# Copies of weight sums on the other DMA queue, an earlier biased input and a tile of its own for the centred block

## The chip, the cores and the metric

The kernel runs on one core of a Trainium2 chip. The metric is the device time of one execution in microseconds (us). Before the change three runs gave 747.36, 748.40 and 749.13 us; the median is 748.4. TensorE (PE) multiplies matrices, VectorE (DVE) and ScalarE (ACT) do the elementwise work, GpSimd (POOL) does little arithmetic here and issues DMAs, and SyncE (SP) only issues DMAs. SP's DMAs go through the queue that the profile calls q1 (hardware_dynamic), POOL's through q0 (software_dynamic).

## The reference

One layer on an input x of 1024 steps by 1024 channels, all in float32:

```python
h = x @ w_in + b_in                        # split: xa, za, xb, zb, ga, gb
xa = causal_depthwise_conv4(xa)
ya = rg_lru(xa) * silu(za)                 # two block-diagonal gates, a scan over time
yb = multi_scale_pool(xb) * silu(zb)       # running means, a projection per group
merged = sigmoid(ga) * (ya @ w_proj_a) + sigmoid(gb) * (yb @ w_proj_b)
y = merged @ w_out + b_out
out = layer_norm(alpha * x + y) * ln_gain + ln_bias     # alpha = 2 ** 0.25
```

## The kernel before

**The products.** The input projection, the two merge projections and the output projection are each done as a two by two block scheme with seven block products instead of eight (Strassen's, in Winograd's form). Such a scheme needs sums of weight blocks and of input blocks. Each operand is split into a high and a low part by a cast on ACT (names ending in h) and a difference on DVE (names ending in l), and each block product is three matmul passes: high by high, low by high, high by low.

**The stages.** The first stage goes over 24 groups of the input projection, the list `order` of L601 to L604: G0, A0, G1 to A5, G6, A6, A7, G7 (the branch A is the recurrence, G are the merge gates), then B0 to B7 (the pooling). A group loads its weights (tiles ra and rb), casts them (wah, wal and so on), multiplies (PSUM tiles a, c, e) and hands its results on. A further small weight, gr, 64 KB, holds the gates' blocks of an A group: it is loaded by SP (`load_g`) and cast to gh on ACT and gl on DVE. The branches' outputs ya and yb are stored to DRAM. Next come the merge products (PSUM tiles pa, pc and pe; `load` at L1231 fetches weights such as wa1r and inputs such as xa1r, `cast` at L1241 splits them into oh and ol), and last the output products (oa, oc, oe) with the norm. In the output phase eight blocks of 128 rows, zt[s] (z in the profile), are loaded from DRAM tiles xb, which hold x + b_out / alpha; `o_add` (L1419) adds each product to them and `o_norm` (L1433) normalises each block.

**Sums in DRAM.** Sums that only feed later loads are made in DRAM by DMA, without an engine: `summed` (L673) makes a tile by a copy of the first term and one accumulating DMA for each further term (`add_to`, L670; accumulation always goes through POOL). It serves `weight_sums` (p1a to p4a and p1b to p4b), `output_sums` (L690; p1o to p4o, four tiles of 1 MB with one copy and one addition each), and `input_sums1` and `input_sums2` (t1 to t4 of each branch). `biased_input` (L702) does the same for xb: two halves of the bias row go to SBUF, are multiplied by 1 / alpha on ACT and stored to a DRAM row; then four tiles xb of 1 MB get a copy of x and the addition of the broadcast row. All copies and additions are issued by POOL.

**When they are issued.** Each copy and each addition is a job in the list `jobs`. After each group from the third on, `run_jobs` (L663) pops two jobs (three in B groups). It first lets ACT copy one column of that group's last result (pace) and POOL copy that (paced), so that POOL goes on only when the group is there. A DMA that needs another's result waits for it at its issue, and holds what POOL issues behind it. `output_sums` and the first input sums are appended when ya's first half is complete, `input_sums2("a")` and `biased_input` after the last A group.

**The order.** The engines' programs are not written in the order of the code: `Plan` (L162 to L392) collects all operations, gives each a due time worked back from PE's order, and lays out the engines' programs from estimated durations. PE and POOL keep the written order. SP, ACT and DVE are sorted by due time; SP issues a load at most 25 us (LEAD) ahead of its due time. What runs is fixed by these orders and by semaphores. All operations are emitted at L394, so the profile tells them apart by tiles alone.

Of the kernel before, what the change touches and what calls it, by code (L numbers as in the profile page):

```python
# [11 lines left out]
F32 = mybir.dt.float32  # L12
F32R = mybir.dt.float32r
AF = mybir.ActivationFunctionType
ALU = mybir.AluOpType
# [391 lines left out]
def layer_kernel(ctx: ExitStack, tc: tile.TileContext, xq, x, w_in, par, wg, w_pool, wpa, wpb, w_out, rows, out):  # L407
# [235 lines left out]
    def both(t, m1):  # L643
        for sl in HALF:
            V.tensor_tensor(t[:, sl], t[:, sl], m1, ALU.add)
# [17 lines left out]
    def run_jobs(n, i=None, t=None):  # L663
        if jobs and i is not None:
            A.copy(pace[:, i:i + 1], t[:, 0:1])
            nc.gpsimd.tensor_copy(paced[:, i:i + 1], pace[:, i:i + 1])
        for _ in range(min(n, len(jobs))):
            jobs.pop(0)()

    def add_to(t, u):  # L670
        nc.gpsimd.dma_start(t, u, accum_op=ALU.add, max_dma_last_dim=2048)

    def summed(name, *terms):  # L673
        t = dram.tile([KQ, P, H], F32, tag=name, name=name)
        jobs.append(lambda: nc.gpsimd.dma_start(t, terms[0]))
        for u in terms[1:]:
            jobs.append(lambda: add_to(t, u))
        return t

    def weight_sums(n, w):  # L680
        a11, a12, a21, a22 = (w[KQ * i:KQ * i + KQ, :, KQ * k:KQ * k + KQ, :].rearrange("n p k m -> n p (k m)")
                              for i in range(2) for k in range(2))
        p1 = summed(f"p1{n}", a21, a22)
        p3 = summed(f"p3{n}", a11, a21)
        p2 = summed(f"p2{n}", a11, p1)
        src["w", n] = {1: a11, 2: a12, 4: a22, 5: p1, 6: p2, 7: p3, 3: summed(f"p4{n}", a12, p2)}
# [3 lines left out]
    def output_sums():  # L690
        a11, a12, a21, a22 = (w_out[H * k:H * (k + 1), H * i:H * (i + 1)].rearrange("(q p) n -> q p n", p=P)
                              for i in range(2) for k in (1, 0))
        p1 = summed("p1o", a21, a22)
        p3 = summed("p3o", a11, a21)
        p2 = summed("p2o", a11, p1)
        src["w", "o"] = {1: a11, 2: a12, 4: a22, 5: p1, 6: p2, 7: p3, 3: summed("p4o", a12, p2)}


    xb_d = [dram.tile([2 * P, D], F32, tag=f"xb{i}", name=f"xb{i}") for i in range(4)]
    bias_d = dram.tile([1, D], F32, tag="bias", name="bias")  # L700

    def biased_input():  # L702
        for sl in HALF:
            t = epool.tile([1, H], F32, tag="e", name=f"bias_{sl.start}")
            nc.sync.dma_start(t, rows[0:1, sl])
            A.mul(t, t, 1.0 / ALPHA)
            nc.sync.dma_start(bias_d[:, sl], t)
        for i in (2, 3, 0, 1):
            jobs.append(lambda i=i: nc.gpsimd.dma_start(xb_d[i], x[2 * P * i:2 * P * (i + 1), :]))
            jobs.append(lambda i=i: add_to(xb_d[i], bias_d.to_broadcast((2 * P, D))))  # L710


    def input_sums1(n):
# [46 lines left out]
    def a_gates(c, xc, xh, xl, sz):  # L760
        gh, gl = gw[c]
        if c + 1 < NK:
            load_g(c + 1)

        r, i = kt(f"r{c}"), kt(f"i{c}")
        for h in range(2):
            pg = [bank(f"ps_g{c}_{h}_{n}") for n in range(2)]
            for k, (w, m) in enumerate(((gh, xh), (gh, xl), (gl, xh))):
                for n in range(2):
                    nc.tensor.matmul(pg[n], w[HEAD[n], :], m[HEAD[n], HALF[h]], start=k == 0, stop=k == 2)  # L770
            for t, half, ps, s, cb in ((r, LO, pg[0], LO, C_BR), (r, HI, pg[1], HI, C_BR),
                                       (i, LO, pg[0], HI, C_BI), (i, HI, pg[1], LO, C_BI)):
                A.activation(t[half, HALF[h]], ps[s], AF.Sigmoid, bias=par_sb[s, cb + c:cb + c + 1])

        a = kt(f"a{c}")
        A.activation(a, r, AF.Exp, scale=sc_a[:, c:c + 1])
        t = r
        A.activation(t, r, AF.Tanh, scale=sc_t[:, c:c + 1])
        V.tensor_tensor(i, i, xc, ALU.mult)
        V.scalar_tensor_tensor(i, a, 1.0, i, ALU.add, ALU.mult)  # L780
        V.scalar_tensor_tensor(a, a, 1.0, t, ALU.add, ALU.mult)
        V.tensor_scalar(a, a, -1.0, 1.0, ALU.mult, ALU.add)
        A.activation(t, t, AF.Sqrt)
        V.tensor_tensor(i, i, t, ALU.mult)
        hs = t
        V.tensor_tensor_scan(hs, a, i, 0.0, ALU.mult, ALU.add)
        V.tensor_tensor(hs, hs, sz, ALU.mult)
        A.mul(hs[:, negative(c)], hs[:, negative(c)], -1.0)
        store_y("a", c, hs)
        if c == KQ - 1:  # L790
            input_sums1("a")
            output_sums()
        elif c == NK - 1:
            input_sums2("a")
            biased_input()


    sg_d = {sec: dram.tile([NK, P, S], F32, tag=f"sg{sec}", name=f"sg{sec}") for sec in (GA, GB)}
# [349 lines left out]
    due, pools, last, ends, W = {}, {}, [], [], {}  # L1148
    weight_sums("a", wpa)
    weight_sums("b", wpb)  # L1150
    for i in range(1, len(order)):
        kind, c = order[i]
        if i == 1:
            W[2] = load_group(2, w_next, ("4", "75", "63"))
        elif i + 1 < len(order):
            W[i + 1] = load_group(i + 1)
        if kind == "B" and c % 2 == 1:
            load_wp(c // 2)
        if i == 1:
            tiles = tiles0  # L1160
        elif kind == "A":
            tiles, takes = a_outputs(c)
        elif kind == "B":
            tiles, takes = b_outputs(c)
        else:
            finish, takes = g_outputs(GA if c < 4 else GB, c % 4)
        if i > 1:
            g = Group(f"{kind}{c}", W.pop(i), X, *takes)

        def heads(at=pools):  # L1170
            for f in at.pop(i, []):
                f()

        def between():
            heads(due)
            if prev_m3:
                prev_m3()
            if prev_end and i > 2:
                prev_end()

        if i == 1:
            prev_m3 = None
        elif i >= len(order) - 2:
            g.sums(between, heads)
            prev_m3 = None
            last.append(g)
        else:
            g.m1()
            g.m2()
            if i == 2:  # L1190
                rest = first_rest()
                next(rest)
            g.m7()
            between()
            g.m6()
            if i == 2:
                next(rest)
                prev_end()
            g.m4()
            heads()  # L1200
            g.m5()
            prev_m3 = g.m3
        if i >= 2:
            run_jobs(3 if kind == "B" else 2, i, g.t7)
        if kind == "A":
            def prev_end(c=c, tiles=tiles, i=i):
                front = a_front(c, *tiles)
                due.setdefault(i + 2, []).append(lambda: a_gates(c, *front, tiles[1]))
        elif kind == "B":
            def prev_end(c=c, tiles=tiles, i=i):  # L1210
                for _ in b_front(c, *tiles):
                    pass
                if c % 2 == 1:
                    pools.setdefault(i + 2, []).append(lambda: b_pool(c // 2))
        else:
            prev_end = finish
        if i >= len(order) - 2:
            ends.append((c, *tiles))
            prev_end = None
# [213 lines left out]
    def o_norm(s):  # L1433
        sd = const.tile([P, 1], F32, name=f"sd{s}")
        sls = [slice(e * H, (e + 1) * H) for e in range(2)]
        if s == last:
            mv = const.tile([P, 2], F32, name=f"mv{s}")
            V.bn_aggr(mv, stats)
            A.activation(sd, mv[:, 1:2], AF.Sqrt, bias=eps)
            mean, op = mv[:, 0:1], ALU.subtract  # L1440
        else:
            nm, var = (const.tile([P, 1], F32, name=f"{n}{s}") for n in ("nm", "var"))
            V.tensor_scalar(nm, acc[:, 2 * s:2 * s + 1], acc[:, 2 * s + 1:2 * s + 2], -1.0 / D, ALU.add, ALU.mult)
            sq = kt(f"sq{s}")
            A.activation(sq, zt[s], AF.Square, bias=nm, accum_out=var)
            A.activation(sd, var, AF.Sqrt, bias=eps, scale=1.0 / D)
            mean, op = nm, ALU.add
        for sl in sls:
            V.scalar_tensor_tensor(zt[s][:, sl], zt[s][:, sl], mean, g_row[:, sl], op, ALU.mult)
        V.reciprocal(sd, sd)  # L1450
        if s in BY_DMA:
            A.mul(zt[s], zt[s], sd)
            add_to(out[s * P:(s + 1) * P, :], zt[s])
            return
        for sl in sls:
            V.scalar_tensor_tensor(zt[s][:, sl], zt[s][:, sl], sd, be_row[:, sl], ALU.mult, ALU.add)
            nc.sync.dma_start(out[s * P:(s + 1) * P, sl], zt[s][:, sl])

    def o_product(ps, j, g, start, stop, sl=slice(0, H)):
        for q in range(KQ):  # L1460
# [106 lines left out]
```

## Time and profile before

| what | value |
|---|---|
| three runs | 747.36, 748.40, 749.13 us |
| the profiled execution, its own time | 748.43 us |
| its span, first to last instruction | 746.6 us |
| mean granted TensorE clock | 0.995 |
| PE busy | 733.2 us, 98% |
| DVE, ACT, POOL busy | 600.0, 457.4, 76.0 us |
| q1 (SP) | 102.06 MB, 38.9% of 16 engines' span |
| q0 (POOL) | 55.58 MB, 34.7% |

A row of a timeline gives start, length, engine, operation, the tile written and those read, sizes, and in brackets how long the engine was idle before and what ended that. In the rows of a chain start and length come first. In a table of windows the columns are the busy time of PE, its weight loads, DVE, ACT and POOL with the number of instructions, then PE's granted clock, the DMA share and GB/s. A row of a DMA queue gives packets, MB and the share of the time of 16 engines in that window; a row of DMA issues the number, KB each and the median time from issue to landing.

### The profile page before, as it was taken

To read this page: it belongs to the slowest core of one execution; us is meant where nothing else is said; L and a number is where in the kernel's file an instruction comes from. 1 tells how busy PE (TensorE), PEld (TensorE's weight loads), DVE (VectorE), ACT (ScalarE), POOL (GpSimd) and SP (SyncE) were. 2 spreads that over 40 slices of the span, in tenths; PEclk is the share of its full clock that TensorE was granted. 3 is DMA by queue.
4 is the path that set the end of the run, shared out by engine and by line. 5 is a ranking of instruction groups with operands and counts; after the bars stand their busy time and mean duration, and the time that the engine had idled before them with its cause. 6 is when DMAs were issued, how large, how long until landed. Compare 5 with 4: busy or idle time off the path is not lost.

```text
span 746.6 us, 8782 instructions
## 1 busy us (share of the span) xinstructions
PE 733.2 (98%) x3248; PEld 599.9 (80%) x3248; DVE 600.0 (80%) x746; ACT 457.4 (61%) x585; POOL 76.0 (10%) x125
## 2 busy tenths in 40 slices
PE   8999999999999999999999999999999999999995
PEld 6888888888787888788888888887888888888884
DVE  7999696969596968787977768856978886999766
ACT  7676959686868777788744445526563546324472
POOL 0171011111101011010012111110001000000021
PEclk9999999999999999999999999999999999999998
DMA  9337868676836957667187978999699998759365
GB/s 336 116 117 175 225 171 227 140 241 167 237 97 169 346 152 207 180 183 191 51 196 156 246 190 231 226 321 396 216 323 331 305 270 292 269 203 244 119 108 118
DMA packets 62435, 158.46 MB, mean 212 GB/s; under 512 B 4276, under 2 KB 7476, under 8 KB 62264
## 3 DMA queue, kind: packets, MB, share of 16 engines
q1 hardware_dynamic: 41880, 102.06, 38.9%
q0 software_dynamic: 19968, 55.58, 34.7%
q8 instruction: 25, 0.41, 0.2%
q10 hardware_dynamic: 544, 0.26, 0.1%
q14 instruction: 18, 0.15, 0.1%
HBM read 136.91 MB, written 76.55 MB: 286 GB/s over the span
## 4 chain that ended last, share of the span: by engine, by line
PE 95%; DMA 3%; DVE 1%; ACT 0%; DVEq 0%; ACTq 0%; issue 0%
PE a_A L394 11%; PE a_G L394 10%; PE a_B L394 10%; PE oa L394 6%; PE pa_b L394 6%; PE c_B L394 6%; PE c_A L394 6%; PE pa_a L394 5%; PE c_G L394 5%; PE ps_pool L394 3%; PE pc_b L394 3%; PE pc_a L394 3%; PE e_A L394 3%; PE ps_s L394 3%; PE oc L394 3%; PE e_G L394 3%
## 5 line engine op out<-in xcount | busy, mean ns | idle before, releaser
L394 ACT ACT_TABLE_LOAD x38 | 48.8, 1283 | 2.7 <-issue 2.0
L394 DVE TENSOR_TENSOR i<-i,xc 128x1024 f32<-128x1024 f32 x8 | 9.8, 1225 | 28.3 <-ACT i L394 28.3
L394 DVE SCALAR_TENSOR_TENSOR xc<-xp,par_sb,xc 128x1024 f32<-128x1024 f32 x24 | 30.7, 1279 | 0.3
L394 POOL COPY paced<-pace 128x1 f32<-128x1 f32 x21 | 12.1, 574 | 174.1 <-ACT pace L394 174.1
L394 PE MATMUL pa_a<-oh,oh 128*128 128x512 f32 x64 | 25.7, 402 | 1.3 <-ACT oh L394 1.3
L394 PE MATMUL pa_a<-oh,ol 128*128 128x512 f32 x64 | 25.6, 400 | 0.5 <-DVE ol L394 0.5
L394 PE MATMUL pa_a<-ol,oh 128*128 128x512 f32 x64 | 25.5, 398 | 0.0
L394 PE MATMUL pa_b<-oh,oh 128*128 128x512 f32 x64 | 24.9, 389 | 0.0
L394 PE MATMUL pa_b<-ol,oh 128*128 128x512 f32 x64 | 24.9, 389 | 0.0
L394 PE MATMUL pa_b<-oh,ol 128*128 128x512 f32 x64 | 24.9, 389 | 0.0
L394 ACT ACTIVATE r<-ps_g,par_sb 64x512 f32<-64x512 f32 x32 | 21.9, 684 | 2.1 <-PE ps_g L394 1.2
L394 ACT ACTIVATE i<-ps_g,par_sb 64x512 f32<-64x512 f32 x32 | 21.9, 684 | 1.9 <-DVE r L394 1.4
L394 ACT ACTIVATE zb<-zb,par_sb 128x1024 f32<-128x1024 f32 (+1 forms) x16 | 15.0, 938 | 13.0 <-DVE zb L394 12.9
L394 PE MATMUL c_A<-x64h,wd_A 128*128 128x512 f32 x64 | 21.0, 389 | 0.0
L394 PE MATMUL c_B<-x64h,wd_B 128*128 128x512 f32 x64 | 21.0, 389 | 0.0
L394 PE MATMUL ps_pool<-mixh,wp 128*128 128x512 f32 x64 | 20.6, 394 | 0.0
L394 POOL DMA_DIRECT2D out<-z x6 | 7.1, 1190 | 124.7 <-ACT z L394 124.7
L394 PE MATMUL e_B<-x,wah_B 128*128 128x512 f32 x64 | 19.7, 389 | 0.0
L394 PE MATMUL e_A<-x,wah_A 128*128 128x512 f32 x64 | 19.7, 389 | 0.0
L394 PE MATMUL c_G<-x64h,wd_G 128*128 128x512 f32 x56 | 18.4, 389 | 0.0
L394 DVE TENSOR_TENSOR_SCAN r<-a,i 128x1024 f32<-128x1024 f32 x8 | 18.3, 2283 | 0.1
L394 PE MATMUL e_G<-x,wah_G 128*128 128x512 f32 x56 | 17.2, 389 | 0.0
(522 smaller groups left out, 2544.6 us busy)
## 6 DMA issues: line engine op xcount, KB each, us to landing
sg<-sg SPq DMA_DIRECT2D x16, 512.0 KB, 4.9
ra_A<-in_w_in SPq DMA_DIRECT2D x8, 512.0 KB, 9.5
rb_A<-in_w_in SPq DMA_DIRECT2D x8, 512.0 KB, 6.6
ya<-r SPq DMA_DIRECT2D x8, 512.0 KB, 5.0
ra_B<-in_w_in SPq DMA_DIRECT2D x8, 512.0 KB, 6.0
rb_B<-in_w_in SPq DMA_DIRECT2D x8, 512.0 KB, 5.3
yb<-zb SPq DMA_DIRECT2D x8, 512.0 KB, 6.5
xb<-bias POOLq DMA_DIRECT2D x4, 1024.0 KB, 12.6
```

The source lines that it names most:

```text
L394: getattr(getattr(nc, t.op[0]), t.op[1])(*a, **k)
```

## The change

Four things change.

1. The copies of p1o, p3o, p2o and p4o are issued by SP; the copy and POOL's addition are one job.
2. `biased_input` is called twice. The first call, ahead of the groups' loop, makes the bias row and appends xb2 and xb3 behind the weight sums; the second, where the call was, appends xb0 and xb1. The copies of x into xb are issued by SP, and copy and addition are one job.
3. `run_jobs` pops two jobs up to i = 9 and three from then on, instead of two, and three in B groups.
4. In `o_norm` the centred block is written to a tile y of its own, except for the last block, and scaled there; z stays as it was.

```diff
-    def summed(name, *terms):
+    def summed(name, *terms, copy=None):
         t = dram.tile([KQ, P, H], F32, tag=name, name=name)
+        if copy:
+            def first(a=terms[0], b=terms[1]):
+                copy.dma_start(t, a)
+                add_to(t, b)
+            jobs.append(first)
+            return t
         jobs.append(lambda: nc.gpsimd.dma_start(t, terms[0]))
...
-        p1 = summed("p1o", a21, a22)
-        p3 = summed("p3o", a11, a21)
-        p2 = summed("p2o", a11, p1)
-        src["w", "o"] = {1: a11, 2: a12, 4: a22, 5: p1, 6: p2, 7: p3, 3: summed("p4o", a12, p2)}
+        p1 = summed("p1o", a21, a22, copy=nc.sync)
+        p3 = summed("p3o", a11, a21, copy=nc.sync)
+        p2 = summed("p2o", a11, p1, copy=nc.sync)
+        src["w", "o"] = {1: a11, 2: a12, 4: a22, 5: p1, 6: p2, 7: p3, 3: summed("p4o", a12, p2, copy=nc.sync)}
...
-    def biased_input():
-        for sl in HALF:
+    def biased_input(blocks):
+        for sl in HALF if not src.get("bias") else ():
+            src["bias"] = True
             t = epool.tile([1, H], F32, tag="e", name=f"bias_{sl.start}")
             nc.sync.dma_start(t, rows[0:1, sl])
             A.mul(t, t, 1.0 / ALPHA)
             nc.sync.dma_start(bias_d[:, sl], t)
-        for i in (2, 3, 0, 1):
-            jobs.append(lambda i=i: nc.gpsimd.dma_start(xb_d[i], x[2 * P * i:2 * P * (i + 1), :]))
-            jobs.append(lambda i=i: add_to(xb_d[i], bias_d.to_broadcast((2 * P, D))))
+        for i in blocks:
+            def both(i=i):
+                nc.sync.dma_start(xb_d[i], x[2 * P * i:2 * P * (i + 1), :])
+                add_to(xb_d[i], bias_d.to_broadcast((2 * P, D)))
+            jobs.append(both)
...
-            biased_input()
+            biased_input((0, 1))
...
     weight_sums("b", wpb)
+    biased_input((2, 3))
...
-            run_jobs(3 if kind == "B" else 2, i, g.t7)
+            run_jobs(2 if i < 10 else 3, i, g.t7)
...
+        y = zt[s] if s == last else xt(f"y{s}", F32, (P, S))
         for sl in sls:
-            V.scalar_tensor_tensor(zt[s][:, sl], zt[s][:, sl], mean, g_row[:, sl], op, ALU.mult)
+            V.scalar_tensor_tensor(y[:, sl], zt[s][:, sl], mean, g_row[:, sl], op, ALU.mult)
         V.reciprocal(sd, sd)
         if s in BY_DMA:
-            A.mul(zt[s], zt[s], sd)
-            add_to(out[s * P:(s + 1) * P, :], zt[s])
+            A.mul(y, y, sd)
+            add_to(out[s * P:(s + 1) * P, :], y)
             return
         for sl in sls:
-            V.scalar_tensor_tensor(zt[s][:, sl], zt[s][:, sl], sd, be_row[:, sl], ALU.mult, ALU.add)
-            nc.sync.dma_start(out[s * P:(s + 1) * P, sl], zt[s][:, sl])
+            V.scalar_tensor_tensor(y[:, sl], y[:, sl], sd, be_row[:, sl], ALU.mult, ALU.add)
+            nc.sync.dma_start(out[s * P:(s + 1) * P, sl], y[:, sl])
```

PE's order is the same in both kernels. Three places show what moves on the others. The number behind a tile's name tells tiles of one name apart, and the names behind "waits" are semaphores: of an engine, or of DMAs issued by SP (DMAHW) or by POOL (DMASW).

SP's program around the load of gr that was issued at 268.28, before: a store of ya, the weights ra_G and rb_G of a coming group and gr, then two loads of gates (sg), the weights of the group behind and the next gr.

```order
L394 DMA ya<-r_2019 128x1024 [waits DMAHW1_49,Activation_49]
L394 DMA ra_G_2291<-in_w_in 128x1024 [waits DMAHW3_49,DMAHW2_49]
L394 DMA rb_G_2311<-in_w_in 128x1024 [waits DVE_49]
L394 DMA gr_2400<-in_wg 128x128 [waits DMAHW4_49]
L394 DMA sg_1824<-sg_2_2158 128x1024 [waits DMAHW5_49,Activation_49]
L394 DMA sg_1824<-sg_6_2240 128x1024 [waits DMAHW6_49]
L394 DMA ra_B_2462<-in_w_in 128x1024 [waits DMAHW7_49,DMAHW0_49,DVE_49]
L394 DMA rb_B_2481<-in_w_in 128x1024 [waits DVE_49,Activation_49]
L394 DMA gr_2557<-in_wg 128x128 [waits DMAHW1_49]
```

The same place now:

```order
L394 DMA ya<-r_2030 128x1024 [waits DMAHW7_49,Activation_49]
L394 DMA p1o<-in_w_out 512x512 [waits DMAHW0_49]
L394 DMA ra_G_2301<-in_w_in 128x1024 [waits DMAHW1_49]
L394 DMA p3o<-in_w_out 512x512 [waits DMAHW2_49]
L394 DMA rb_G_2323<-in_w_in 128x1024 [waits DMAHW3_49,DVE_49]
L394 DMA p2o<-in_w_out 512x512 [waits DMAHW4_49]
L394 DMA gr_2421<-in_wg 128x128 [waits DMAHW5_49]
L394 DMA sg_1833<-sg_2_2170 128x1024 [waits DMAHW6_49,Activation_49]
L394 DMA sg_1833<-sg_6_2245 128x1024 [waits DMAHW7_49]
L394 DMA ra_B_2480<-in_w_in 128x1024 [waits DMAHW0_49,DVE_49]
L394 DMA p4o<-in_w_out 512x512 [waits DMAHW1_49]
L394 DMA rb_B_2501<-in_w_in 128x1024 [waits DMAHW2_49,DVE_49,Activation_49]
```

The copies of p1o, p3o and p2o have come between the store of ya and the load of gr, and p4o's stands ahead of rb_B; the next gr follows behind this piece.

POOL's program from the third pair of xb to the first sums of the branch B, before:

```order
L394 DMA xb_3655<-in_x 16x16384 [waits DMASW5_49]
L394 DMA xb_3655<-bias 256x2x512 [waits DMASW6_49,DMASW5_49]
L394 DMA xb_3810<-in_x 16x16384
L394 COPY paced<-pace 128x1 [waits Activation_49]
L394 DMA xb_3810<-bias 256x2x512 [waits DMASW7_49,DMASW0_49]
L394 COPY paced<-pace 128x1 [waits Activation_49]
L394 DMA t1b<-yb 512x512 [waits DMAHW7_49,DMAHW6_49,DMAHW3_49]
L394 DMA t1b<-yb 512x512 [waits DMASW2_49,DMASW1_49]
L394 DMA t3b<-yb 512x512
L394 COPY paced<-pace 128x1 [waits Activation_49]
L394 DMA t2b<-t1b 16x16384 [waits DMASW4_49,DMASW2_49]
L394 DMA t4b<-t1b 16x16384
```

The same place now, from the last addition for t4a on:

```order
L394 DMA t4a<-ya 512x512 [waits DMASW5_49]
L394 DMA xb_3109<-bias 256x2x512 [waits DMAHW0_49]
L394 DMA xb_3112<-bias 256x2x512 [waits DMAHW1_49,DMASW0_49]
L394 COPY paced<-pace 128x1 [waits Activation_49]
L394 DMA t1b<-yb 512x512 [waits DMAHW7_49,DMAHW6_49,DMAHW3_49]
L394 DMA t1b<-yb 512x512 [waits DMASW2_49,DMASW1_49]
L394 DMA t3b<-yb 512x512 [waits DMASW3_49]
L394 COPY paced<-pace 128x1 [waits Activation_49]
L394 DMA t2b<-t1b 16x16384 [waits DMASW4_49,DMASW2_49]
L394 DMA t4b<-t1b 16x16384
```

Two additions to xb are left of the eight copies and additions that POOL had issued ahead of t1b; the other two stand far ahead in POOL's program, in front of the first sums of ya, and all copies are SP's.

DVE's program at the end of the output phase, where the block before the last is normalised and the last product is added to the last block, before:

```order
L394 TENSOR_SCALAR nm_5905<-o_acc 128x1 [waits DVE_49]
L394 SCALAR_TENSOR_TENSOR z_5273<-z_5273,nm_5905,row_5455 128x512 [waits Activation_49]
L394 SCALAR_TENSOR_TENSOR z_5273<-z_5273,nm_5905,row_5455 128x512
L394 TENSOR_TENSOR z_5279<-z_5279,oc_5594 128x512 [waits PE_49]
L394 RECIPROCAL sd_5916<-sd_5916 128x1 [waits Activation_49]
L394 SCALAR_TENSOR_TENSOR z_5273<-z_5273,sd_5916,row_5457 128x512 [waits DVE_49]
L394 TENSOR_TENSOR z_5279<-z_5279,oe_0_5921 128x256 [waits PE_49]
L394 SCALAR_TENSOR_TENSOR z_5273<-z_5273,sd_5916,row_5457 128x512
```

The same place now:

```order
L394 TENSOR_SCALAR nm_5901<-o_acc 128x1 [waits DVE_49]
L394 SCALAR_TENSOR_TENSOR y_5904<-z_5263,nm_5901,row_5445 128x512 [waits DVE_49]
L394 SCALAR_TENSOR_TENSOR y_5904<-z_5263,nm_5901,row_5445 128x512
L394 RECIPROCAL sd_5915<-sd_5915 128x1 [waits Activation_49]
L394 SCALAR_TENSOR_TENSOR y_5904<-y_5904,sd_5915,row_5447 128x512 [waits DVE_49]
L394 TENSOR_TENSOR z_5269<-z_5269,oc_5584 128x512 [waits PE_49]
L394 SCALAR_TENSOR_TENSOR y_5904<-y_5904,sd_5915,row_5447 128x512
L394 TENSOR_TENSOR z_5269<-z_5269,oe_0_5921 128x256 [waits PE_49]
```

The centring step now writes y and waits for DVE alone instead of ACT; the reciprocal follows directly and has the wait for ACT; adding oc to the last block has moved behind the first scaling step.

## The prediction

> **What bounds the kernel now.** I read the page, the chain that ended last, then timelines around the places where the chain leaves TensorE (PE). The page first.
>
> ```profile
> span 746.6 us, 8782 instructions
> PE 733.2 (98%) x3248; PEld 599.9 (80%) x3248; DVE 600.0 (80%) x746; ACT 457.4 (61%) x585; POOL 76.0 (10%) x125
> ```
>
> PE is busy for 733.2 of 746.6 us, so a gain can only come out of the 13.4 us that remain, or out of matmuls at a lower clock; the order of the matmuls is not changed. The span is 1.8 us below that run's 748.43, and that run is the median of the three (748.4), so I sum against 748.43. A measurement of this kernel tells about 0.2% (1.5 us) from no change.
>
> In the chain one entry belongs to a transfer, at the start of the merge phase, followed by blocks of matmuls like the second line (start, length).
>
> ```profile
> 490.02 14.01 DMA wa1r<-in_wpa
> ...
> 513.27 10.88 PE pe_a L394 x48
> ```
>
> The timelines of ACT and PE there (start, length, engine), and the granted clock in a window behind the gaps (0.50, the column ahead of the DMA share):
>
> ```profile
> 504.06 1.04 ACT L394 CAST oh<-wa1r 128x1024 fp32r<-128x1024 f32 x1 [9.80 <-DMA wa1r<-in_wpa]
> ```
>
> ```profile
> 503.43 0.39 PE L394 MATMUL pa_a<-oh,ol 128*128 128x512 f32 x1
> 505.15 0.50 PE L394 MATMUL pa_a<-oh,oh 128*128 128x512 f32 x1 [1.34 <-ACT oh L394]
> ...
> 506.42 0.63 PE L394 MATMUL pa_a<-oh,ol 128*128 128x512 f32 x1 [0.53 <-DVE ol L394]
> ...
> 509.83 0.49 PE L394 MATMUL pa_a<-ol,oh 128*128 128x512 f32 x1
> ```
>
> ```profile
> 508.00:510.00 2.00, 2.00 (x6) 1.54 (x6) 1.97 (x2) 0.51 (x1) 0.00 (x0) 0.50 1.40 553
> ```
>
> Matmuls start every 0.227 us at full clock (10.88 us for 48 in the chain's row). The next after 503.43 was due at 503.66 and came at 505.15, 1.5 us late; at 509.83 the eleventh behind it starts, due at 503.66 + 10 x 0.227 = 505.9. So the stall costs **4.0 us**: 1.9 of idle time (the brackets) and 2.1 of matmuls 0.43 us apart.
>
> **The stall at the merge.** Why did 0.5 MB take 14 us? The queues from 488 to 503 (MB, share of 16 engines), and what POOL had to do first:
>
> ```profile
> q0 software_dynamic: 760, 1.97, 53.9%
> q1 hardware_dynamic: 1296, 2.74, 51.4%
> ```
>
> ```profile
> 448.02 4.12 SPq L394 DMA_DIRECT2D yb<-zb  x2
> ```
>
> ```profile
> yb<-zb SPq DMA_DIRECT2D x4, 512.0 KB, 2.9
> ```
>
> ```profile
> 468.49 1.55 POOL L394 DMA_DIRECT2D xb<-bias  x1 [12.85 <-DMA xb<-in_x]
> 469.53 2.35 POOL L394 DMA_DIRECT2D t1b<-yb  x1
> ...
> 502.41 0.51 POOL L394 DMA_DIRECT2D t2b<-t1b  x1 [12.96 <-DMA t1b<-yb]
> ```
>
> POOL's queue (q0) shares the engines with SyncE's (q1), because t1b could only start behind the last xb pair, at 469.53. The change takes all xb pairs from there: t1b then waits only for the yb stores (issued by 448.02 + 4.12, landing in 2.9 us: about 455). From t1b to t2b it was 32.9 us here; the like work for t1a, with little beside it, took 229.06 to 248.54, 19.5 us:
>
> ```profile
> 229.06 0.65 POOL L394 DMA_DIRECT2D t1a<-ya  x1 [14.78 <-DMA ya<-r]
> ...
> 248.54 0.52 POOL L394 DMA_DIRECT2D t2a<-t1a  x1 [9.64 <-DMA t1a<-ya]
> ```
>
> So t2b is issued between 475 and 488, and with t2b and t4b, copies of 1 MB like t1b, q0 is idle some 10 us later, between 485 and 498 (an estimate: t1a's first copy took 8 us here). q1 moved 0.183 MB/us in the window above and 1.61 MB in 67.7% of 7 us, 0.34 MB/us, where it had the engines to itself (225 to 232, quoted below). wa1r, issued at 490.02 with 14 x 0.183 = 2.6 MB up to its end, lands at 497.5 if q0 is idle, at 501.2 if q0 is busy until 498. From the cast it was 1.1 us to the first matmul and 2.4 to the first with ol (504.06 to 505.15 and 506.42), the latter due at 503.66 + 2 x 0.227 = 504.1, so 501.7 is in time: **-4.0 us** (bounds -4.0 and 0, taken -4.0 since both ends make it). Half of this price rests on the low clock being the gaps' doing; the 0.50 right behind the only gaps of this phase speaks for that. The Trainium skill's "TensorE: Matmul & The Clock Gate" (Part 1: The HAM clock gate) lets the clock fall after an idle window of some 3.4 us, longer than the 1.34 and 0.53 us here; by that rule the last rival below would hold, and no run here shows a gap of that length.
>
> **The norm's own tile.** The tail of DVE and ACT:
>
> ```profile
> 733.25 0.21 DVE L394 TENSOR_SCALAR nm<-o_acc 128x1 f32<-128x1 f32 x1
> 734.83 1.42 DVE L394 SCALAR_TENSOR_TENSOR z<-z,nm,row 128x512 f32<-128x512 f32 x2 [1.37 <-ACT sq L394]
> 736.16 0.68 DVE L394 TENSOR_TENSOR z<-z,oc 128x512 f32<-128x512 f32 x1
> ...
> 736.95 0.75 DVE L394 SCALAR_TENSOR_TENSOR z<-z,sd,row 128x512 f32<-128x512 f32 x1
> ```
>
> ```profile
> 734.83 0.29 ACT L394 ACTIVATE sd<-var,eps 128x1 f32<-128x1 f32 x1
> ```
>
> The centring step waits 1.37 us for ACT's Square only because it overwrites z. Written to y it starts at 733.5 and ends at 734.9; the reciprocal now waits for sd (734.83 + 0.29 = 735.12) and goes at 735.2, and the same work follows from there, with z<-z,oc (0.68 us, 0.6 to the next start) behind it instead of ahead. Before, the step behind the reciprocal went at 736.95; now at 735.4, with 0.6 still to do: **-0.95 us** (bounds -0.7 and -1.4: with a wake-up more, or the whole wait). What is late next is sd on ACT, then DVE itself.
>
> **Fewer copies, early bias.** Two 1x512 products on ACT move to about 41 us, behind a 2 KB load on SP; SP's store of the product, and the loads queued behind it, wait for that. ACT was idle soon after:
>
> ```profile
> 331.38 1.13 ACT L394 ACTIVATE bias<-bias 1x512 f32<-1x512 f32 x2
> ```
>
> ```profile
> 48.15 1.05 ACT L394 CAST wch_G<-ra_G 128x1024 fp32r<-128x1024 f32 x1 [0.80 <-PE e_G L394]
> ```
>
> Of the 1.13 us 0.80 fit there, and the chain runs through PE alone at that place: **0** (0 to +1, and nothing below, as only work is added). Five pace copies vanish, at a place where PE waits for nothing: 0.
>
> **The copies on SP's queue.** This decides. In the new order SP issues xb, xb ahead of rb_A and gr at 226; p1o, p3o and p2o, 1 MB each, between ya, ra_G, rb_G and gr at 265.7; and p4o ahead of rb_B and the next gr. The other two xb go ahead of ra_B and rb_B at 371, whose cast came at 388.89, for matmuls at 408.12: room for 2.1 MB more, 0.
>
> ```profile
> 388.89 1.06 ACT L394 CAST wah_B<-ra_B 128x1024 fp32r<-128x1024 f32 x1 [1.39 <-PE e_B L394]
> ```
>
> The other two places hang on gr; the first and the last of its casts are 245.2 and 304.8. At 226 there is 19 us of room, 2.1 MB more ahead, and q0 idle until the first xb has landed, as its addition waits for it: 0 (0 to +3). At 265.7 there is less, and ACT takes its work in order.
>
> ```profile
> L394 ACT CAST gh<-gr x3: 277/281/294, 245.2 to 304.8; 128x128 fp32r<-128x128 f32 x3
> ```
>
> ```profile
> 265.70 0.33 SPq L394 DMA_DIRECT2D ya<-r  x1
> ...
> 268.28 0.42 SPq L394 DMA_DIRECT2D gr<-in_wg  x1
> ```
>
> ```profile
> 285.10 0.28 ACT L394 CAST gh<-gr 128x128 fp32r<-128x128 f32 x1
> ...
> 287.66 0.57 ACT L394 COPY m_A<-a_A 128x512 f32<-128x512 f32 x1
> ...
> 298.40 0.59 ACT L394 COPY u_A<-a_A 128x512 f32<-128x512 f32 x1 [1.09 <-PE a_A L394]
> ```
>
> ```profile
> 295.48 0.39 PE L394 MATMUL a_A<-x64h,wch_A 128*128 128x512 f32 x1
> ...
> 300.92 0.39 PE L394 MATMUL a_A<-x57h,wbh_A 128*128 128x512 f32 x1
> ```
>
> ```profile
> ra_G<-in_w_in SPq DMA_DIRECT2D x1, 512.0 KB
> ...
> gr<-in_wg SPq DMA_DIRECT2D x1, 64.0 KB, 4.1
> ```
>
> gr had ya, ra_G and rb_G of 0.52 MB each ahead of it and landed in 4.1 us; now it has 3 x 0.52 + 3 x 1.05 = 4.7 MB. If q1 has the engines alone (first row), at 0.34 MB/us that is 13.9 us, and gr lands at 265.7 + 13.9 + 2 = 281.6, in time. Beside a busy q0 q1 moved 0.183 MB/us (488 to 503): 25.7 us, landing 293.4; and in 239.45 to 256.70 (second and third row) 1.94 MB in 17.25 us, 0.112 MB/us: 42 us, 309.
>
> ```profile
> q1 hardware_dynamic: 541, 1.61, 67.7%
> ```
>
> ```profile
> q0 software_dynamic: 816, 3.37, 74.8%
> q1 hardware_dynamic: 527, 1.94, 30.5%
> ```
>
> q0 is busy in this stretch: POOL, two bias additions ahead of t1a now, still has the sums with t1a to do, and p1o's and p3o's additions start as soon as their copies land. I take 0.17 MB/us: 27.8 us, landing **R = 295.5**. Then ACT stands from 285.1 to 295.5. m_A's copy, 2.6 us behind gh, is for the matmuls at 295.48, free until R = 292.3; u_A, with the 3.8 us that ACT waited for PE on the way taken out, comes 10.1 us behind gh's start and is for those at 300.92, free until R = 290.8; with part of these waits kept, 288.8. So PE loses R - 289.8 = 5.7 us (4.7 to 6.7), and, as at the merge, about 2.1 more at the lower clock. The next gr has 3.2 MB more ahead: at 0.17, 18.6 us later, 314.1, against a cast at 304.8 + 5.7 with the 3.7 us that ACT had to spare: nothing (0 to +4); I take 0.7. Sum: **+8.5 us** (0 to +18).
>
> What queues share is told by the Trainium skill, "DMA: Bandwidth & Descriptors", Queues, rings and completion order: each engine goes round robin between the queues it has work for, packet by packet. That gives SP's queue no right of way, as the falling rate from 0.34 to 0.183 shows.
>
> **Sum.** 748.43 - 4.0 - 0.95 + 0 + 8.5 = **752.0 us**.
>
> **Rivals.**
> - The loads come in time (the other side): R is at most 289, since q0 may be idle between t4a and p1o's addition. It needs 4.7 MB in 21 us, 0.22 MB/us, between the two measured rates. Then 748.43 - 4.95 = 743.5 us, faster. For it: q1 alone needs 14 us. Against: the loads of 239.45 to 256.70 had far less.
> - A half stall: R of 290 to 294 with a loss of 1 to 6 us: 744.5 to 749.5.
> - The stall at the merge stays (t1b is held by another wait, or wa1r is late through q1's own loads): only the norm is won, 747.5 us, no change, if the loads come in time.
> - The low clock at 508 is not the gaps': 748.43 - 1.9 - 0.95 = 745.6 us with the loads in time.
>
> **Chances.** Forecast (R above 294): 0.50, its own range 749.8 to 759. Loads in time: 0.28. Half stall: 0.14, half of it below 746.9 and so faster, half within 0.2%. Merge stall stays: 0.05. Low clock: 0.03. Faster 0.28 + 0.07 + 0.03 = 0.38; same 0.07 + 0.05 = 0.12; slower 0.50. The range reaches from the loads in time, 743, to the sum with R = 301 (743.5 + 11.2 + 2.1 + 2), 759; it leaves out the upper end of a late gr and some of the lower.
>
> **What would show it.** Right: a wait of ACT's gh for gr of several us at 285 to 300, gr landing 25 us or more behind its issue, new waits of PE for m_A or u_A and a lower clock behind them; wa1r landing within 10 us and no wait of PE at the merge; the centring step right behind nm. Wrong: gr landing by 289, when the rival at 743.5 holds; wa1r as late as before; or waits for gr at 245 or 370.

## The result and the profile after

The changed kernel takes 760.53 us (median of 6 runs, 757.03 to 762.63) against 748.1 us before (6 runs); the ratio is 1.0165 with a 95% interval of 1.0138 to 1.0192. It is slower, as forecast, by 12.4 us instead of 3.6, and lies above the range of 743 to 759. The profiled execution after is the longest of the six (762.63 us); its span is 760.8 us, 14.2 more than before.

Where these 14.2 us are is read from places on the chain that both kernels have (start, length): the first matmuls behind the first block, the last group before the branch B, the merge phase and the last output block. First before, then after.

```profile
29.07 2.72 PE a_A L394 x12
...
334.46 2.94 PE a_G L394 x12
...
513.27 10.88 PE pe_a L394 x48
...
729.76 2.73 PE oe L394 x12
```

```profile
30.44 2.72 PE a_A L394 x12
...
353.63 2.95 PE a_G L394 x12
...
528.37 10.88 PE pe_a L394 x48
...
744.82 2.73 PE oe L394 x12
```

After stands behind before by 1.37, 19.17, 15.10 and 15.06 us. So 17.80 us are lost between 30 and 353, 4.07 are won up to the merge, nothing changes in the output products, and behind the last of these blocks 0.86 are won (14.2 at the span's end). The first 1.37 are not the change's: the granted clock fell just behind the first matmul of this execution, here from 8 to 12 us (before, then after; the clock is the column of 1.00 and 0.57), and in the profiles of the runs below, with the change or without, only e2 has its matmuls as far apart there (0.43 us).

```profile
8.00:12.00 4.00, 4.00 (x19) 3.30 (x19) 3.67 (x5) 3.25 (x4) 0.00 (x0) 1.00 1.06 409
```

```profile
8.00:12.00 4.00, 4.00 (x12) 3.14 (x12) 3.92 (x5) 3.23 (x4) 0.00 (x0) 0.57 1.05 407
```

The waits of PE name the loss; the two of pa_a at the merge (1.3 and 0.5 us before) are not there any more.

```profile
PE a_A L394 <- ACT m_A L394: 14.4, 1, 14.4
...
PE a_A L394 <- ACT u_A L394: 1.1, 1, 1.1
```

SP's timeline and ACT's show why m_A was late:

```profile
267.02 0.33 SPq L394 DMA_DIRECT2D ya<-r  x1
267.40 0.50 SPq L394 DMA_DIRECT2D p1o<-in_w_out  x1
267.95 0.80 SPq L394 DMA_DIRECT2D ra_G<-in_w_in  x1
268.80 1.25 SPq L394 DMA_DIRECT2D p3o<-in_w_out  x1
270.15 1.28 SPq L394 DMA_DIRECT2D rb_G<-in_w_in  x1
271.48 0.50 SPq L394 DMA_DIRECT2D p2o<-in_w_out  x1
272.02 17.73 SPq L394 DMA_DIRECT2D gr<-in_wg  x1
```

```profile
308.16 0.30 ACT L394 CAST gh<-gr 128x128 fp32r<-128x128 f32 x1 [21.65 <-DMA gr<-in_wg]
...
310.73 0.57 ACT L394 COPY m_A<-a_A 128x512 f32<-128x512 f32 x1
```

gr, 64 KB, stands behind 4.7 MB. Its issue alone takes 17.73 us, and it lands at 308.1, 41 us after the store of ya at the head of this piece. ACT stands for 21.65 us with everything behind gh. The 14.4 and 1.1 us of idle PE are 15.5 of the 17.8. Another 1.9 is the clock, which was at half when PE went on at 311.35 and full again by 316: the twelve matmuls behind the gap took 4.64 us, and before 2.72. The last 0.4 are not accounted for.

```profile
308.00:310.00 2.00, 0.00 (x0) 0.00 (x0) 0.29 (x1) 1.81 (x3) 0.00 (x0) 0.50 1.07 311
...
314.00:316.00 2.00, 2.00 (x8) 1.56 (x7) 2.00 (x2) 2.00 (x4) 0.00 (x0) 0.70 1.08 240
316.00:318.00 2.00, 2.00 (x10) 1.68 (x9) 1.93 (x4) 0.29 (x1) 0.00 (x0) 1.00 0.85 209
```

What POOL had to do at that time (its timeline, after): the sums with t1a, which were issued at 229 to 254 before, are now issued at 251 to 280. The second addition of the bias landed 13.0 us behind its issue, at 263.4, ahead of gr's load; what crosses that load is the work that had to stand behind it.

```profile
236.48 1.57 POOL L394 DMA_DIRECT2D xb<-bias  x1 [20.86 <-DMA xb<-in_x]
250.33 1.53 POOL L394 DMA_DIRECT2D xb<-bias  x1 [12.29 <-issue]
251.22 1.33 POOL L394 DMA_DIRECT2D t1a<-ya  x1
...
266.20 1.03 POOL L394 DMA_DIRECT2D t1a<-ya  x1 [13.43 <-DMA t1a<-ya]
266.86 1.03 POOL L394 DMA_DIRECT2D t3a<-ya  x1
279.36 0.51 POOL L394 DMA_DIRECT2D t2a<-t1a  x1 [11.47 <-DMA t1a<-ya]
...
279.97 0.50 POOL L394 DMA_DIRECT2D t4a<-t1a  x1
```

The tail of DVE after: the centring step follows nm directly, the reciprocal waits 0.25 us for sd, and from nm to the aggregate it is 6.26 us; before it was 7.13 (733.25 to the second fence's 740.38).

```profile
748.31 0.21 DVE L394 TENSOR_SCALAR nm<-o_acc 128x1 f32<-128x1 f32 x1
748.56 1.42 DVE L394 SCALAR_TENSOR_TENSOR y<-z,nm,row 128x512 f32<-128x512 f32 x2
750.22 0.16 DVE L394 RECIPROCAL sd<-sd 128x1 f32<-128x1 f32 x1 [0.25 <-ACT sd L394]
...
754.57 0.26 DVE L394 BATCH_NORM_AGGREGATE mv<-stats 128x2 f32<-128x24 f32 x1
```

```profile
740.38 0.26 DVE L394 BATCH_NORM_AGGREGATE mv<-stats 128x2 f32<-128x24 f32 x1
```

### The profile page after: what moved, and what is told of

It is laid out like the page before. It is cut to its first block, busy times and chain, and to the rows that moved or that the text cites. A ratio compares the mean times of both kernels' runs of the same rounds, so it can differ in the third digit from the quotient of the medians.

```text
span 760.8 us, 8775 instructions
## 1 busy us (share of the span) xinstructions
PE 734.7 (97%) x3248; PEld 601.1 (79%) x3248; DVE 601.8 (79%) x746; ACT 456.9 (60%) x580; POOL 66.3 (9%) x112
## 4 chain that ended last, share of the span: by engine, by line
PE 90%; SPq 4%; DMA 3%; DVE 2%; ACT 1%; issue 0%; DVEq 0%; ACTq 0%
PE a_B L394 11%; PE a_G L394 9%; PE a_A L394 9%; PE oa L394 6%; PE pa_a L394 6%; PE pa_b L394 6%; PE c_B L394 6%; PE c_G L394 5%; PE c_A L394 4%; SPq L394 4%; PE ps_s L394 3%; PE ps_pool L394 3%; PE pc_b L394 3%; PE pc_a L394 3%; PE e_B L394 3%; PE oc L394 3%
## 5 line engine op out<-in xcount | busy, mean ns | idle before, releaser
L394 PE MATMUL a_A<-x64h,wch_A 128*128 128x512 f32 x32 | 13.3, 417 | 14.4 <-ACT m_A L394 14.4
L394 ACT ACTIVATE zb<-zb,par_sb 128x1024 f32<-128x1024 f32 (+1 forms) x16 | 15.0, 938 | 14.2 <-DVE zb L394 14.0
L394 PEld LDWEIGHTS a_A<-x64h,wch_A 128*128 128x128 f32 x32 | 6.5, 204 | 16.2 <-ACT m_A L394 14.8
L394 ACT CAST xch<-xc 128x1024 fp32r<-128x1024 f32 x8 | 8.4, 1053 | 16.6 <-DVE xc L394 16.6
```

What stands on the lines that cost most here:

```text
L394: getattr(getattr(nc, t.op[0]), t.op[1])(*a, **k)
```

## The experiments

Two theories were set against each other. A: gr is late because of what stands ahead of it in SP's own queue, at a rate that POOL's transfers set. B: gr is late because the early additions to xb moved POOL's work into the stretch from 266 to 306. Times in us; each is a median beside runs of the kernel before on the same chip.

| run | median | ratio to before, 95% interval | gr lands |
|---|---|---|---|
| the change | 760.53 | 1.0138 to 1.0192 | 308.1 |
| e1 tile of its own alone | 748.60 | 0.9969 to 1.0018 | |
| e2 output copies on POOL | 743.56 | 0.9881 to 0.9943 | 282.1 |
| e3 all copies on POOL | 744.89 | 0.9898 to 0.9956 | 283.2 |
| e4 gr ahead, copies wait | 765.83 | 1.0175 to 1.0253 | 287.7 |
| e5 no additions to p | 752.45 | 1.0032 to 1.0070 | 297.5 |
| e6 no early additions to xb | 743.25 | 0.9904 to 0.9953 | 288.0 |
| e7 gr ahead of the copies | 747.96 | 0.9978 to 1.0024 | 281.2 |
| e8 copies apart | 743.21 | 0.9911 to 0.9946 | 285.7 |
| e9 copies apart, no own tile | 743.86 | 0.9908 to 0.9948 | |
| e10 output copies on SP alone | 749.52 | 0.9984 to 1.0023 | |
| e11 two of the four copies on SP | 751.53 | 1.0023 to 1.0079 | 295.1 |
| e12 xb's copies on POOL | 749.81 | 0.9998 to 1.0032 | 294.9 |

Landings are the issue plus the transfer's time to landing, or, where ACT waited, the start of its cast.

**e1.** The kernel before with change 4 alone.

```diff
+        y = zt[s] if s == last else xt(f"y{s}", F32, (P, S))
...
-            V.scalar_tensor_tensor(zt[s][:, sl], zt[s][:, sl], mean, g_row[:, sl], op, ALU.mult)
+            V.scalar_tensor_tensor(y[:, sl], zt[s][:, sl], mean, g_row[:, sl], op, ALU.mult)
```

> The kernel before with the centred block in a tile of its own, nothing else. Both theories (A: the loads stand behind SP's copies; B: the moved xb work crowds the engines from 266 to 306 us) expect the tail alone: 0.95 us less than before (0.7 to 1.4), DVE's centring step right behind nm, the wait of PE at the merge as before.

The interval is wider than the 0.95 us in question, so the time says nothing. The profile shows the tail as after the change (6.26 us from nm to the aggregate).

**e2 and e3.** In e2 the copies of the output sums stay in one job with the addition, but POOL issues them; in e3 those of x into xb too.

```diff
-        p1 = summed("p1o", a21, a22, copy=nc.sync)
+        p1 = summed("p1o", a21, a22, copy=nc.gpsimd)
...
-                nc.sync.dma_start(xb_d[i], x[2 * P * i:2 * P * (i + 1), :])
+                nc.gpsimd.dma_start(xb_d[i], x[2 * P * i:2 * P * (i + 1), :])
```

> The changed kernel with the four copies of the output sums issued by POOL, as one job with the addition; all else changed. Theory A: no wait of ACT for gr, no wait of PE for m_A, no wait at the merge: 748.1 - 4.0 - 0.95 = 743.2 us. Theory B: the same bytes cross in the same stretch and xb's additions are still early, so gr is still late by several us: 750 us or more.

> As the run with the output copies on POOL, and the copies of x into xb on POOL too: nothing is left on SP, the order of the jobs is the changed one. Both theories on the merge: what wins there is that t1b no longer stands behind xb, not the queue of the copies, so the wait for wa1r stays away. A: 743.2 us, the same as with xb on SP, within 1 us. B: 750 or more.

e2 met A's number. e3, expected within 1 us of it, came out 1.3 above, with ranges that overlap and far from B's 750. gr of e2 landed 12.5 us behind its issue, though POOL's sums lay as late as after the change, and ACT did not wait for it:

```profile
269.59 1.84 SPq L394 DMA_DIRECT2D gr<-in_wg  x1
```

```profile
DMA to landing us min/median/max: 12.5/12.5/12.5
```

So the loss of 17.8 us needs the copies on SP. And e3 shows that the stall at the merge goes without a single copy on SP: what counts there is when xb is done.

**e4.** p1o, p3o and p2o were put on SP behind gr instead of ahead of it. In this version the copies of p1o and p3o also come behind POOL's additions to these tiles in the emitted order and wait for them, so that these sums lack their second term.

```diff
+            late = [t for t in order if t.eng == "SP" and t.op[1] == "dma_start" and t.args[0].tile.name in ("p1o", "p3o", "p2o")]
+            order = [t for t in order if t not in late]
...
+            order[k:k] = late
             for t in order:
```

> The changed kernel with p1o, p3o and p2o moved on SP's program from between ya and gr to right behind that gr; bytes, POOL and all else unchanged. Theory A: gr lands at about 267 + 1.6 MB / 0.115 = 281 us and ACT does not wait for it; the same bytes are now ahead of the next gr (304.8 in the kernel before), which landed at about 317 and would hold ACT some 7 us there: 748 to 753 us. Theory B: this gr is late as before, 758 to 762 us.

The time, 765.83 us, is neither theory's number. The first gr came in time (287.7, PE does not wait), for A. But SP stood at p1o's copy until POOL's addition had landed, with the gates, weights and next gr behind it; that gr came at 328.8, and the whole got slower than the change:

```profile
267.98 0.55 SPq L398 DMA_DIRECT2D gr<-in_wg  x1
292.05 0.50 SPq L398 DMA_DIRECT2D p1o<-in_w_out  x1
```

**e7.** The same with POOL's additions held behind the copies: move puts SP's copies of these tiles behind a load, the first (0) or a later one at or behind their old place whose name begins so, and emits POOL's tasks, in their order, once what they need is emitted.

```diff
+            order = move(order, ("p1o", "p3o", "p2o"), "gr", 0)
             for t in order:
```

> The changed kernel with p1o, p3o and p2o moved on SP from between ya and gr to right behind that gr, POOL's additions still behind the copies and in their order. Theory A: this gr lands by 288 and PE does not wait for it; the next gr has the same bytes ahead as before and lands at about 317, where ACT wants it at 306: ACT waits some 10 us and PE 5 to 10, 748 to 755 us. Theory B: the first gr is late as in the changed kernel, 760 us.

A held: the first gr is cast at 285.21 without a wait, the next waits 7.35 us for the bytes that are now ahead of it, and PE loses 3.5 us at u_G and some clock. The net is that of before.

```profile
285.21 0.28 ACT L413 CAST gh<-gr 128x128 fp32r<-128x128 f32 x1
...
312.60 0.30 ACT L413 CAST gh<-gr 128x128 fp32r<-128x128 f32 x1 [7.35 <-DMA gr<-in_wg]
```

**e5 and e6.** SP's program word for word as after the change; e5 leaves out the four additions to p1o to p4o, e6 the two early additions to xb2 and xb3.

```diff
             for t in order:
+                if t.eng == "POOL" and t.kw.get("accum_op") and t.args[0].tile.name in ("xb2", "xb3"):
+                    continue
```

> The changed kernel without the four additions to p1o, p3o, p2o and p4o (these sums lack their second term); SP's program word for word as in the changed kernel. Theory A, in the form that gr is late because of what stands ahead of it on SP and because POOL's transfers share the engines: POOL's queue is done with t4a at about 290, the rest of the copies then has the engines alone, gr lands at 295 to 300 instead of 308, 750 to 754 us. If SP's order alone counts: 308 and 760. If the additions alone count: gr by 290 and 743.

> The changed kernel without the two early additions of the bias to xb2 and xb3 (half of the input lacks b_out); SP's program as in the changed kernel. The sums with t1a then start some 15 us earlier and are nearly done at 267. Theory A with sharing: gr lands at 295 to 300, 750 to 754 us. SP's order alone: 308 and 760. If the moved additions alone make gr late (theory B): 743.

e5 came out as A with sharing has it. e6 gave 743.25, B's number, and missed what A with sharing had forecast (295 to 300): with three copies still ahead of gr and without two additions 30 us earlier, gr landed at 288.0, and PE did not wait.

```profile
288.06 0.30 ACT L396 CAST gh<-gr 128x128 fp32r<-128x128 f32 x1 [2.85 <-DMA gr<-in_wg]
```

So neither theory is enough alone. The queues from 265 to 289 (MB, share of 16 engines), after the change and in e6:

```profile
q0 software_dynamic: 841, 3.87, 60.7%
q1 hardware_dynamic: 965, 2.40, 31.2%
```

```profile
q1 hardware_dynamic: 2416, 5.74, 72.6%
q0 software_dynamic: 528, 1.05, 24.1%
```

SP's queue moves 2.40 MB in 24 us beside 3.87 MB of POOL's, and 5.74 MB beside 1.05. Beside a busy POOL the two have 965 and 841 packets, nearly one for one; by the Trainium skill, "DMA: Bandwidth & Descriptors" (Queues, rings and completion order), the engines go round robin between queues by packets, and these rows fit that, if the profile counts the same packets, which no run here shows. Bytes alone do not set the rate: in e12, below, SP's queue got nearly twice as much over the same stretch beside almost as many bytes of POOL's, in far fewer packets, and POOL's queue was all but empty from 277 to 285.

```profile
q1 hardware_dynamic: 1895, 4.48, 54.3%
q0 software_dynamic: 509, 3.39, 45.2%
```

In e6 POOL's queue moved next to nothing from 265 to 277. So A, with the rate set by how long POOL has work in its queue at that time, explains both, and e2 as well; POOL's work came to that time by the early additions. This form of A was found from the runs, not forecast.

**e8.** The changed kernel with SP's copies apart, one group's loads between each two; p1o's now stands behind the gr in question.

```diff
+            order = move(order, ("p1o",), "gr", 0)
+            order = move(order, ("p3o",), "gr", 1)
+            order = move(order, ("p2o",), "rb_B", 1)
+            order = move(order, ("p4o",), "rb_B", 2)
             for t in order:
```

> The changed kernel with SP's four copies apart: p1o behind the gr of 268, p3o behind the next gr, p2o and p4o behind the two rb_B after that. Theory A: no load of gr has more than one copy of 1 MB ahead (2.6 MB and 64 KB in 20 us), so none is late by more than the room of 3 us: 743 to 745 us, like the kernel with these copies on POOL. Theory B: gr late at 285 by several us still, 748 or more.

743.21 us: faster than before by 0.7%, level with the copies on POOL. gr landed 17.8 us behind its issue, ACT waited 1.1 us, PE not at all.

```profile
285.75 0.30 ACT L416 CAST gh<-gr 128x128 fp32r<-128x128 f32 x1 [1.09 <-DMA gr<-in_wg]
```

**e9.** The same with the centring step on z again.

```diff
-        y = zt[s] if s == last else xt(f"y{s}", F32, (P, S))
...
-            V.scalar_tensor_tensor(y[:, sl], zt[s][:, sl], mean, g_row[:, sl], op, ALU.mult)
+            V.scalar_tensor_tensor(zt[s][:, sl], zt[s][:, sl], mean, g_row[:, sl], op, ALU.mult)
```

> The kernel with the four copies apart, without the norm's own tile (the centred block overwrites z again). Its runs lie closer together than those of before, so the tile's worth can be read against 743.2 us of the kernel with the copies apart: theory of the tail 744.15 us (0.7 to 1.4 more); if DVE's wait for ACT was hidden by something else, 743.2.

0.65 us more, in runs of 743.52 to 744.26 against 742.67 to 743.78. But the two were taken on different chips, and beside the kernel before on each the ratios are 0.9928 and 0.9929, so the time does not show what the tile is worth. The profile does: e9 has the wait back, and 7.13 us from nm to the aggregate, where e8 has 6.26.

```profile
729.10 0.22 DVE L416 TENSOR_SCALAR nm<-o_acc 128x1 f32<-128x1 f32 x1
730.68 1.42 DVE L416 SCALAR_TENSOR_TENSOR z<-z,nm,row 128x512 f32<-128x512 f32 x2 [1.37 <-ACT sq L416]
...
736.23 0.26 DVE L416 BATCH_NORM_AGGREGATE mv<-stats 128x2 f32<-128x24 f32 x1
```

**e10.** The kernel before with copy=nc.sync for the output sums, the copies still jobs of their own.

```diff
-        jobs.append(lambda: nc.gpsimd.dma_start(t, terms[0]))
+        jobs.append(lambda: (copy or nc.gpsimd).dma_start(t, terms[0]))
```

> The kernel before with the copies of the output sums on SP and nothing else: they stay jobs of their own, so the planner puts them apart, one ahead of each gr at most, and xb stays late. Theory A with sharing: gr is not late, the stall at the merge is as before: 748 us, no change. SP's copies cost by themselves: 752 or more.

No change: one copy ahead of a gr cost nothing here, and with xb late the stall at the merge stays (PE's waits of this run).

```profile
PE pa_a L394 <- ACT oh L394: 2.2, 1, 2.2
...
PE pa_a L394 <- DVE ol L394: 0.5, 1, 0.5
```

**e11.** The changed kernel with copy=nc.gpsimd for p2o and p4o alone.

```diff
-        p2 = summed("p2o", a11, p1, copy=nc.sync)
+        p2 = summed("p2o", a11, p1, copy=nc.gpsimd)
```

> The changed kernel with p2o's and p4o's copies on POOL: gr has 3.7 MB ahead instead of 4.7. Theory A with sharing, by the rates of the changed kernel (0.10 MB/us up to 289, 0.21 behind it): gr lands at about 297 instead of 308, PE loses some 4 us and the lower clock: 748 to 753 us. A threshold elsewhere (three copies fill something, two don't): 743.

gr landed at 295.1 and the time lies between: no sign of a threshold between two copies and three; the landing moved with the bytes ahead.

```profile
295.10 0.30 ACT L394 CAST gh<-gr 128x128 fp32r<-128x128 f32 x1 [10.02 <-DMA gr<-in_wg]
```

**e12.** The changed kernel with the copies of x into xb on POOL (the second edit of e3 alone).

```diff
-                nc.sync.dma_start(xb_d[i], x[2 * P * i:2 * P * (i + 1), :])
+                nc.gpsimd.dma_start(xb_d[i], x[2 * P * i:2 * P * (i + 1), :])
```

> The changed kernel with the copies of x into xb on POOL, still early, in the same jobs; p1o to p4o on SP as in the changed kernel. Theory A with sharing: POOL's two copies push the sums with t1a back by some 6 us more, so gr is at least as late as in the changed kernel: 758 to 766 us. If it was the early copies on SP that made gr late: 743 to 750.

The expectation of A with sharing failed: 749.81 us, at the upper end of what was given for the early copies on SP as the cause, and gr came at 294.9, 13 us earlier than after the change. POOL issued its first copy for xb at 214.01, as soon as its group was there; SP, after the change, only at 227.98, behind the store of ya and a load.

```profile
214.01 0.53 POOL L394 DMA_DIRECT2D xb<-in_x  x1
...
236.07 1.32 POOL L394 DMA_DIRECT2D t1a<-ya  x1
```

```profile
227.98 1.44 SPq L394 DMA_DIRECT2D xb<-in_x  x2
```

So the copies that SP issued later held POOL: after the change its first addition waited 20.86 us for one of them, and the second addition and t1a came behind that, t1a at 251.22 instead of 236.07. Of the 20.1 us by which gr came later after the change than in e6, 13.2 are not there in e12; the other 6.9 are left with additions still ahead of t1a, which e6 starts at 229.12.

## Why the prediction was right in kind and wrong in size

- **The stall at the merge**, forecast -4.0: 4.07 won. t1b started at 474.97, 9.7 us earlier than before once the 15.1 are taken off, and the load of wa1r landed in 5.9 us instead of 14.0. e3 and e10 show that the stall hangs on when xb is done. The low clock and the gaps go together: from 508 to 512 it is 0.74 before and 0.57 in e10, which have them, and 1.00 in e3, e6 and e8, which do not. The clock was not changed by itself.
- **The norm's own tile**, forecast -0.95: 0.87 from nm to the aggregate, in after against before and in e8 against e9; no time shows it clear of the noise.
- **Early bias and fewer copies**, forecast 0: no wait of PE at 40 to 60 us in the profile after, and no loss in e2 and e8, which have these edits.
- **The copies on SP's queue**, forecast +8.5: 17.8. The mechanism and its place held: gr, gh, m_A, u_A, then the lower clock. The step that failed is the size of one term, "I take 0.17 MB/us": gr's 4.7 MB took 41 us, 0.114 MB/us, instead of the 27.8 of the sum, and landed at 308.1 instead of 295.5. SP's queue moved 3.71 MB in the 36 us from 265 to 301, beside 5.17 of POOL's, and only then had the engines almost to itself. POOL was at work that long because the two early additions, and the copies that they waited for, had put t1a off from 229 to 251; the prediction named these additions ahead of t1a, but did not work out where they put it. e6, where the sums stay early, gave 0.24 over 24 us.
- **The row that came nearest**, 0.112 MB/us of 239.45 to 256.70 with a landing at 309, was among the prediction's three, but its range stopped at R = 301. In that row POOL did the very work (t1a's addition, t3a, t2a) that the change moves into gr's time. That its mean came out so near is partly luck: SP's queue moved 0.14 MB in the first 5.5 us of it and 1.79 MB in the other 11.7, 0.153 MB/us, and after the change the last 7 us of the 41 ran with almost nothing on POOL's queue (0.08 MB).
- By the prediction's own sum with the measured landing (308.1, less the 1.37 of the start: 306.8), PE loses 306.8 - 289.8 = 17.0 and 2.1 of clock, 19.1 against 17.8 measured: what follows from gr's landing was right to 1.3 us. The 0.7 that the sum adds for the next gr did not come: its cast at 327.0 waited for nothing, nor did the one at 246.5.
- **The rival at 743.5** is what the change gives without the crossing: e2 743.56, e6 743.25, e8 743.21.

## What to carry to other kernels

A copy that is off every path still stands in its queue ahead of small loads that are on one: before moving it, add up the bytes ahead of each load behind it, and divide by the rate that the queue has while the other one does the work that it will do then, counting only the time in which both have work, not by a mean between rows. Work out first where the change puts that other work; an early job on a queue in order moves all jobs behind it. And a transfer split over two queues starts when the slower program gets to it: SP's copies were 14 us later than POOL's own, and POOL waited.

## What the runs showed of the hardware

A DMA issue is not always short: gr's took 17.73 us on SP with six transfers of 4.7 MB issued in the 5 us ahead of it, so that later loads were not even queued. With the same order on SP and next to nothing on POOL's queue until 277 (e6) it took 2.21 us. From 265 to 289 SP's queue got 0.10 MB/us beside a busy POOL queue (2.40 MB, POOL 3.87) and 0.24 beside one that moved little (5.74 MB, POOL 1.05).

In the gap of 14.4 us the granted clock was 1.00 from 296 to 300, 0.69 from 300 to 304 and 0.50 behind that; an estimate from the 0.69 puts its fall at 301.5, 4.5 us after the last matmul. PE went on at 311.35 with half its clock, and from 315.29 on its matmuls were 0.23 us apart again, 3.9 us later. The Trainium skill, "TensorE: Matmul & The Clock Gate" (Part 1: The HAM clock gate), has the clock come back after some 3.4 us of work, and this trace agrees within half a microsecond; its idle window of some 3.4 us ahead of a fall fits the long gap, but is not what the start of this execution shows, where the clock fell behind a gap of 1.58 us, while the execution before, with a gap of 1.64, kept it.
